# Sparse attention on one core: the parts of the keys stored once, 128 rows each, and doubled when they are loaded

## The chip, the core and the metric

The kernel runs on one core of one Trainium2 chip. The core has a tensor engine (PE; its weight loads are listed as PEld), a vector engine (DVE), a scalar engine (ACT), GpSimd (POOL) and a sync engine (SP) that here only issues DMAs. Each engine works through its own list of instructions in order. The metric is device time in microseconds for one execution of the whole program.

## The reference, cut to what matters

The program is a block of two transformer layers on 1024 tokens of width 1024, in float32. Layer 1 mixes the tokens in two ways: a sparse attention (`_dsa`, 8 heads of 64 channels; for each query the 256 keys with the largest indexer score) and a state-space scan (S5). The change touches the sparse attention's keys:

```python
def _mixer_dsa_s5(x, w_in, ...):
    h = x @ w_in
    q, k, v, qi, ki, wi, u = _split(h, L1_SPLITS)
    o_dsa = _dsa(q..., k..., v..., qi..., ki, wi * (IDX_HEADS ** -0.5))
    ...
def one_block(args):                       # in _dsa, 128 queries at a time
    logits = jnp.einsum('bqhd,bsd->bqhs', qii, k_idx) * (IDX_DIM ** -0.5)
    score = jnp.einsum('bqhs,bqh->bqs', jax.nn.relu(logits), wi)
    score = jnp.where((key_pos[None, :] <= qpos[:, None])[None], score, -jnp.inf)
    _, sel = lax.top_k(score, topk)        # 256 keys
    s = jnp.einsum('bqhd,bqkhd->bhqk', qi, gather(k, sel)) * (dh ** -0.5)
    p = jax.nn.softmax(jnp.where(sel_ok[:, None], s, -jnp.inf), axis=-1)
    return jnp.einsum('bhqk,bqkhd->bqhd', p, gather(v, sel))
```

## The kernel before, in words

Each float32 factor is split into a high and a low part, so a product is two or three matmuls. The sparse attention does not gather: it computes all causal scores and adds a mask (`bias`, one for each block of 128 queries) that the indexer and the top-256 search made on DVE, ACT and POOL.

`l1_in` (line 1699) projects layer 1's inputs: first values and the scan's inputs, then for each of 4 pairs of heads the queries (`i` = 0) and the keys (`i` = 1), in two halves of 512 tokens. A projection writes 128 rows to PSUM: rows 0 to 63 are the pair's even head, rows 64 to 127 the odd one. ACT copies them as the high part `qkh`, DVE subtracts for the low part `qkl`. All of them go to DRAM and come back later, since on-chip memory is short.

The scores of a head contract over 128 rows. The query operand `qa` holds the head's 64 high rows and its 64 low rows; the key operand must hold the same 64 key rows twice, once against each. `ka` is such a doubled high part, `kl` a doubled low part, each 128 x 512. Before the change the doubling is done by the stores: SP stores each head's 64 rows twice into `dk` (lines 1740 to 1745), two DMAs for each part of 128 rows, and `dsa`'s `load` (line 1759) reads 128 different rows back.

`dsa` runs twice, for the first 512 queries (16 of the 48 key loads) and then for the last 512 (32 of them). The values `vv`, the queries `qa` and the keys are all loaded on POOL's DMA queue; weights (`wr`), the scan's tables (`s5tab`, `ut`) and the stores of `qkh` and `qkl` are issued by SP.

Line 471 stands in every row of the profile, because the program is not issued as written. The functions only record operations. A planner (class `Plan`, `order`, line 242) then simulates the engines with a cost for each operation (line 207) and picks the next one by priority; a DMA's cost there is a fixed issue time of its queue plus its output bytes at 360 bytes a nanosecond. It also assigns on-chip buffers as it goes, and `issue` (line 464) emits the result. So a DMA that is added, removed or made smaller changes the planned times, and with them the order of all that follows on every engine and which buffer each tile gets. On the chip the lists then run in order with semaphore waits; a load waits in POOL's list until the buffer's last reader is done.

Of the kernel before, what the change touches and what calls it, by code (L numbers as in the profile page):

```python
# [11 lines left out]
F32 = mybir.dt.float32  # L12
# [461 lines left out]
P, T, N, KD = 128, 1024, 512, 8  # L474
# [42 lines left out]
class Kern:  # L517
# [1181 lines left out]
    def l1_in(self, x, dq, dk, dv, du):  # L1699

        V, S, A, nc = self.V, self.S, self.A, self.nc
        W = A["l1_fm"]
        us = [self.unit(A["l1_v"][i]) for i in range(4)]
        for b in range(8):
            ps = self.ps1((P, 8, 64))
            bs = slice((b % 4) * P, (b % 4 + 1) * P)
            self.tm(us, lambda k: tuple(t[:, bs] for t in x[k][b // 4]), ps)
            for hg in range(2):
                v = self.slab(F32R, "vv", (P, 4, 2, 64))
                for par in range(2):  # L1710
                    src = ps[:, hg * 4 + par:hg * 4 + 4:2, :]
                    hs, ls = v[:, par::2, par, :], v[:, par::2, 1 - par, :]
                    self.copy(S, hs, src)
                    V.tensor_tensor(ls, src, hs, ALU.subtract)
                nc.scalar.dma_start(out=dv[b, hg], in_=v.rearrange("p a b c -> p (a b c)").bitcast(F32))
            yield
        us = [self.unit(A["l1_u"][i]) for i in range(4)]
        for h in range(2):

            uq = [self.slab(name="ut", shape=(P, 8, 4, 16)) for _ in range(4)]  # L1720
            for j in range(4):
                ps = self.ps1((P, 4, 8, 16))
                self.tm(us, lambda k: tuple(t[:, j::4] for t in x[k][h]), ps)
                for q in range(4):
                    self.copy(S, uq[q][:, :, j, :], ps[:, q])
                    if j == 3:
                        nc.scalar.dma_start(out=du[q, h], in_=uq[q].rearrange("p a b c -> p (a b c)"))
                yield
        for pr in range(4):
            for i, w in enumerate((5 + pr, 9 + pr)):  # L1730
                u = self.unit(W[w])
                for h in range(2):
                    ps = self.ps1()
                    self.dense(x, h, ps, lambda k: self.blk(u, k))
                    hi, lo = self.slab(F32R, "qkh"), self.slab(F32R, "qkl")
                    f = 1.0 if i else 0.125
                    S.activation(hi, ps, AF.Copy, scale=f)
                    V.scalar_tensor_tensor(lo, ps, f, hi, op0=ALU.mult, op1=ALU.subtract)
                    A, B = slice(0, 64), slice(64, 128)
                    st = nc.sync.dma_start  # L1740
                    if i:
                        for part, t in enumerate((hi, lo)):
                            for odd, src in enumerate((A, B)):
                                st(out=dk[pr, h, part, odd].rearrange("(r p) n -> p r n", r=2),
                                   in_=t[src].bitcast(F32)[:, None, :].to_broadcast([64, 2, N]))
                    else:
                        q = dq[pr, h].rearrange("o p n -> (o p) n")
                        st(out=q[0:64], in_=hi[A].bitcast(F32))
                        st(out=q[64:192], in_=lo.bitcast(F32))
                        st(out=q[192:256], in_=hi[B].bitcast(F32))  # L1750
                    yield

    def dsa(self, dq, dk, dv, bias, mix, h):

        V, S, G, TE = self.V, self.S, self.G, self.TE
        val, qk, og = {}, {}, {}
        ld = G.dma_start

        def load(pr):

            if pr % 2 == 0:
                for b in range(4 * h + 4):
                    v = self.slab(F32R, "vv")
                    ld(out=v, in_=dv[b, pr // 2])
                    val[pr // 2, b] = v
            for odd in range(2):
                q = self.slab(F32R, "qa")
                k, l = ([self.slab(F32R, n) for c in range(h + 1)] for n in ("ka", "kl"))
                ld(out=q, in_=dq[pr, h, odd])
                for c in range(h + 1):  # L1770
                    ld(out=k[c], in_=dk[pr, c, 0, odd])
                    ld(out=l[c], in_=dk[pr, c, 1, odd])
                qk[pr, odd] = q, k, l

        def item(hd):
            pr, odd = divmod(hd, 2)

            def prep():
                if odd == 0:
                    load(pr)  # L1780

            def score(qb, w, p):
                q, k, l = qk[pr, odd]
                qs, nm = slice(qb % 4 * P, (qb % 4 + 1) * P), None
                for c in range(0, w, N):
                    n, s = min(N, w - c), self.ps1()
                    m, o = max(n, 256), slice(c, c + n)
                    TE.matmul(s[:, :m], q[:, qs], k[c // N][:, :m], start=True, stop=False)
                    TE.matmul(s[:, :m], q[:, qs], l[c // N][:, :m], start=False, stop=True)
                    last, nm = nm, self.small(1, "nm")  # L1790
                    V.tensor_tensor_reduce(out=p[:, o], in0=s[:, :n], in1=bias[qb][:, o], scale=-1.0,
                                           scalar=-NEG if last is None else last, op0=ALU.add, op1=ALU.min, accum_out=nm)
                return p, nm, -1.0

            def emit(po, sums):
                if not odd:
                    og[h] = self.slab(name="og")
                self.fold(po, odd, og[h], sums)
                if odd:
                    self.dump("o_dsa", og[h], (pr, slice(None), slice(h * N, h * N + N)))  # L1800
                    hi, lo = self.slab(F32R, "mh"), self.slab(F32R, "ml")
                    self.split(og[h], hi, lo, self.by("dsao_h"), self.by("dsao_l"))
                    mix[pr][h] = (hi, lo)

            return hd, h, prep, score, lambda kb: val[hd // 4, kb][:, (hd % 4) * P:(hd % 4 + 1) * P], emit

        yield from self.attention([item(hd) for hd in range(8)])
# [338 lines left out]
def build(ctx, tc, A, out, dbg=None, stop=None):  # L2146

    drams = ctx.enter_context(tc.tile_pool(name="dram", bufs=1, space=DRAM)), {}
    with ExitStack() as first:
        K = Kern(first, tc, A, out, dbg, drams)  # L2150
        program(K, A, out, stop)
        plan = K.nc
        order = plan.order()
        made = K.tiles
    K = Kern(ctx, tc, A, out, dbg, drams, plan.places, made)
    program(K, A, out, stop)
    K.nc.issue(tc, order, plan.took)
    return plan, K.nc


def program(K, A, out, stop=None):
# [19 lines left out]
    dt = K.dram("dt", [4, 2048, P])  # L2181
    dr = K.dram("dr", [KD, P, T])
    dq = K.dram("dq", [4, 2, 2, P, N])
    dk = K.dram("dk", [4, 2, 2, 2, P, N])
    dv = K.dram("dv", [8, 2, P, N])
    du = K.dram("du", [4, 2, P, N])

# [209 lines left out]
```

## Time and profile before

| | |
|---|---|
| time, median of 3 runs | 2381.92 us (2379.25 to 2382.75) |
| time of the profiled execution | 2390.38 us |
| its span (first to last instruction) | 2388.6 us |
| granted TensorE clock, mean | 0.99 |
| PE busy | 2305.8 us, 97% |
| DVE, ACT, POOL busy | 1768.3, 1330.8, 468.2 us (74%, 56%, 20%) |
| DMA moved | 356.59 MB, 174939 packets |
| POOL's DMA queue (q0) | 12672 packets, 23.07 MB, 3.6% of 16 engines |
| SP's DMA queue (q1) | 110704 packets, 243.81 MB, 31.9% |

Read it from the top: PE is busy for 97% of the span, so only work of PE, or time in which PE stands still, can move the end. The page's 40 slices show where it stands still: its digit is 9 everywhere but in the first slice, the last, and two in a row that read 7 and 8, about 1433 to 1552 us. Keys are stored from 1365 to 1470 us and loaded from 1441 to 1597 us.

### The profile page before, as it was taken

Reading aid. Unit: us, or ns where it says so; the run is one execution under the profiler, and the core shown is the slowest. Engines: PE = TensorE matmul, PEld = TensorE weight load, DVE = VectorE, ACT = ScalarE, POOL = GpSimd, SP = SyncE. Lnnn points to the kernel's source line nnn. Section 1 sums busy time; section 2 is a strip of 40 time slices with the busy share of each in tenths; the row PEclk is TensorE's granted clock in tenths of the full one; section 3 lists DMA queues with packets and bytes.
Section 4 is the critical chain, followed back from the end, with each engine's and each line's share of the span. In section 5 each row is a group of like instructions: output and inputs, shape, how many; then the busy total and the mean of one; then the engine's idle time right before and its main releaser. Section 6 shows DMA issues by size and latency. Waiting matters only on the chain. (4 is left out here: it accounts for less than half of the span.)

```text
span 2388.6 us, 33377 instructions
## 1 busy us (share of the span) xinstructions
PE 2305.8 (97%) x11368; PEld 1910.2 (80%) x11368; DVE 1768.3 (74%) x3353; ACT 1330.8 (56%) x2648; POOL 468.2 (20%) x488
## 2 busy tenths in 40 slices
PE   8999999999999999999999997899999999999997
PEld 7788888887878788887778876788877787888887
DVE  8676778468776567579799989885587755675796
ACT  4365567437555554446578775775275455444463
POOL 1252332232000000003211235752320000000021
PEclk9999999999999999999999998999999999999998
DMA  5420001325654585655103469553155546665561
GB/s 182 170 80 1 1 1 51 101 71 162 204 168 154 190 299 194 207 189 203 67 36 115 145 204 282 155 157 127 53 166 187 168 146 212 225 253 193 178 238 36
DMA packets 174939, 356.59 MB, mean 149 GB/s; under 512 B 26784, under 2 KB 39344, under 8 KB 174768
## 3 DMA queue, kind: packets, MB, share of 16 engines
q1 hardware_dynamic: 110704, 243.81, 31.9%
q10 hardware_dynamic: 51392, 87.58, 9.9%
q0 software_dynamic: 12672, 23.07, 3.6%
q8 instruction: 89, 1.46, 0.3%
q14 instruction: 82, 0.67, 0.1%
HBM read 249.66 MB, written 104.73 MB: 148 GB/s over the span
## 5 line engine op out<-in xcount | busy, mean ns | idle before, releaser
L471 PE MATMUL PS<-bh,wb 128*128 128x512 f32 x1792 | 569.0, 395 | 14.5 <-ACT u L471 6.8
L471 PEld LDWEIGHTS PS<-bh,wb 128*128 128x128 f32 x1792 | 335.6, 188 | 105.1 <-ACT u L471 12.6
L471 PE MATMUL PS<-bl,wb 128*128 128x512 f32 x896 | 350.5, 391 | 0.0
L471 PE MATMUL PS<-gl,vh 128*128 128x512 f32 x832 | 324.0, 390 | 2.1 <-DVE gl L471 2.1
L471 PE MATMUL PS<-gh,vh 128*128 128x512 f32 x832 | 322.6, 391 | 2.5 <-ACT vh L471 1.8
L471 PE MATMUL PS<-gh,vl 128*128 128x512 f32 x832 | 323.7, 390 | 0.0
L471 PEld LDWEIGHTS PS<-bl,wb 128*128 128x128 f32 x896 | 169.2, 189 | 34.1
L471 PEld LDWEIGHTS PS<-gh,vh 128*128 128x128 f32 x832 | 156.1, 188 | 37.5 <-ACT vh L471 2.2
L471 PEld LDWEIGHTS PS<-gl,vh 128*128 128x128 f32 x832 | 156.2, 188 | 35.2 <-DVE gl L471 2.5
L471 PEld LDWEIGHTS PS<-gh,vl 128*128 128x128 f32 x832 | 156.2, 188 | 32.3
L471 POOL TENSOR_TENSOR wl<-wr,wh 128x512 fp32r<-128x512 f32 x77 | 120.8, 1584 | 254.9 <-ACT wh L471 154.4
L471 ACT ACTIVATE c<-c 128x512 f32<-128x512 f32 x224 | 140.7, 630 | 50.5 <-DVE c L471 43.5
L471 PE MATMUL PS<-xh,wh 128*128 128x512 f32 (+1 forms) x400 | 155.2, 393 | 12.7 <-ACT xh L471 6.7
L471 POOL TENSOR_TENSOR lnacc<-res,res 128x512 f32<-128x512 f32 (+1 forms) x8 | 9.8, 1223 | 768.1 <-DVE res L471 740.9
L471 ACT ACTIVATE gh<-hr 128x512 fp32r<-128x512 f32 x208 | 129.2, 623 | 52.1 <-PE PS L471 32.6
L471 PE MATMUL PS<-xh,wl 128*128 128x512 f32 (+1 forms) x400 | 154.1, 388 | 2.8 <-POOL wl L471 2.8
L471 DVE TENSOR_TENSOR gl<-hr,gh 128x512 fp32r<-128x512 f32 x208 | 147.7, 711 | 10.9 <-PE PS L471 5.2
L471 PE MATMUL PS<-xl,wh 128*128 128x512 f32 (+1 forms) x400 | 155.3, 389 | 0.0
L471 ACT ACTIVATE wb<-wf 128x512 fp32r<-128x512 f32 x96 | 59.7, 628 | 153.2 <-DMA wf<-in_l_w 94.0
L471 DVE TENSOR_TENSOR wb<-s,wb 128x512 fp32r<-128x512 f32 x128 | 87.8, 688 | 77.0 <-ACT wb L471 76.9
L471 DVE TENSOR_TENSOR vl<-s,vh 128x512 fp32r<-128x512 f32 x112 | 84.2, 754 | 78.5 <-ACT vh L471 39.9
L471 ACT ACTIVATE vh<-s 128x512 fp32r<-128x512 f32 x112 | 70.2, 629 | 108.3 <-PE PS L471 73.2
(371 smaller groups left out, 5497.5 us busy)
## 6 DMA issues: line engine op xcount, KB each, us to landing
wr<-in_l_w SPq DMA_DIRECT2D x118, 512.0 KB, 5.3
hr<-hd SPq DMA_DIRECT2D x208, 256.0 KB, 3.4
wf<-in_l_w SPq DMA_DIRECT2D x80, 512.0 KB, 3.8
hd<-t ACTq DMA_DIRECT2D x128, 256.0 KB, 2.7
hd<-c ACTq DMA_DIRECT2D x96, 256.0 KB, 2.3
wr<-in_l_fm SPq DMA_DIRECT2D x25, 512.0 KB, 5.3
wr<-in_l_wo SPq DMA_DIRECT2D x16, 512.0 KB, 4.5
dx<-res ACTq DMA_DIRECT2D x32, 256.0 KB, 2.4
```

What stands on the lines that cost most here:

```text
L471: r = getattr(queue.real, method)(*a, **k)
```

## The change

`l1_in` stores each part of a key projection as it is, 128 rows, with one DMA: 16 stores to `dk` where there were 32, 4.2 MB where there were 8.4. `load` still issues 48 key loads of 256 KB on POOL's queue, but the source of each is now one head's 64 rows with a first dimension of 2 and a step of 0, so the load reads the 64 rows twice. The buffers that are filled are the same as before.

```diff
--- before.py
+++ after.py
@@ -1740,9 +1740,7 @@
                     st = nc.sync.dma_start
                     if i:
                         for part, t in enumerate((hi, lo)):
-                            for odd, src in enumerate((A, B)):
-                                st(out=dk[pr, h, part, odd].rearrange("(r p) n -> p r n", r=2),
-                                   in_=t[src].bitcast(F32)[:, None, :].to_broadcast([64, 2, N]))
+                            st(out=dk[pr, h, part], in_=t.bitcast(F32))
                     else:
                         q = dq[pr, h].rearrange("o p n -> (o p) n")
                         st(out=q[0:64], in_=hi[A].bitcast(F32))
@@ -1768,8 +1766,8 @@
                 k, l = ([self.slab(F32R, n) for c in range(h + 1)] for n in ("ka", "kl"))
                 ld(out=q, in_=dq[pr, h, odd])
                 for c in range(h + 1):
-                    ld(out=k[c], in_=dk[pr, c, 0, odd])
-                    ld(out=l[c], in_=dk[pr, c, 1, odd])
+                    for part, t in enumerate((k[c], l[c])):
+                        ld(out=t, in_=dk[pr, c, part, 64 * odd:64 * odd + 64][None].to_broadcast([2, 64, N]))
                 qk[pr, odd] = q, k, l
 
         def item(hd):
@@ -2181,7 +2179,7 @@
     dt = K.dram("dt", [4, 2048, P])
     dr = K.dram("dr", [KD, P, T])
     dq = K.dram("dq", [4, 2, 2, P, N])
-    dk = K.dram("dk", [4, 2, 2, 2, P, N])
+    dk = K.dram("dk", [4, 2, 2, P, N])
     dv = K.dram("dv", [8, 2, P, N])
     du = K.dram("du", [4, 2, P, N])
```

The planner reorders the program between about 1366 and 1650 us; elsewhere the lists are the same. Three places are shown: before, then after. In all three the names are tile or DRAM names with buffer numbers, and 64x2x512 is a shape.

SP, around the second to last weight of the pair projections (`wr_3230`, 512 KB) and the stores of a key projection (`dk`):

```order
L471 DMA s5tab_3203_7770<-ds_149 64x512 x2
L471 DMA s5T_3204_7771<-dt_150 128x8x128
L471 DMA dk_153<-qkh_3185_7774 64x2x512 x2
L471 DMA dk_153<-qkl_3186_7776 64x2x512 x2
L471 DMA wr_3230_7778<-in_l1_fm 128x1024
L471 DMA dq_152<-qkh_3217_7780 64x512 x2
L471 DMA dq_152<-qkl_3218_7781 128x512
```

```order
L471 DMA dk_153<-qkh_3169_7765 128x512
L471 DMA s5tab_3203_7767<-ds_149 64x512 x2
L471 DMA dk_153<-qkl_3170_7766 128x512
L471 DMA s5T_3204_7769<-dt_150 128x8x128
L471 DMA wr_3230_7774<-in_l1_fm 128x1024
L471 DMA dk_153<-qkh_3185_7773 128x512
L471 DMA dk_153<-qkl_3186_7776 128x512
```

The weight stood behind the four stores of `qkh_3185` and `qkl_3186`, and now stands ahead of the two that are left of them. Fifteen rows later the last weight, `wr_3261`, moves in the same way from behind the query store `dq<-qkl_3254` to a place ahead of it.

DVE, at the end of the projections; `eq`, `lt`, `cs` and `bias` make the masks of the last four query blocks, `wl` is the low part of the last weight, `wr_3261`:

```order
L471 TENSOR_TENSOR SM_5516<-SM_5516 128x4
L471 TENSOR_SCALAR eq_3177_7819<-sc_2685_7584,SM_5516 128x640
L471 TENSOR_SCALAR lt_3176_7820<-sc_2685_7584,SM_5516 128x640
L471 SCALAR_TENSOR_TENSOR cs_3179_7822<-oneb_6491,eq_3177_7819 128x640
L471 TENSOR_SCALAR eq_3181_7827<-sc_2724_7592,SM_5516 128x768
L471 SCALAR_TENSOR_TENSOR eq_3177_7819<-cs_3179_7822,SM_5516,eq_3177_7819 128x640
L471 SCALAR_TENSOR_TENSOR cs_3183_7831<-oneb_6491,eq_3181_7827 128x768
```

```order
L471 TENSOR_SCALAR SM_5516<-SM_5516 128x4
L471 TENSOR_TENSOR wl_3263_7823<-wr_3261_7813,wh_3262_7819 128x512
L471 TENSOR_TENSOR SM_5516<-SM_5516 128x4
L471 TENSOR_TENSOR wl_3265_7826<-wr_3261_7813,wh_3264_7821 128x512
L471 TENSOR_SCALAR eq_3177_7829<-sc_2685_7584,SM_5516 128x640
L471 TENSOR_SCALAR lt_3176_7831<-sc_2685_7584,SM_5516 128x640
L471 SCALAR_TENSOR_TENSOR cs_3179_7833<-oneb_6491,eq_3177_7829 128x640
```

The two `wl` operations were POOL's before; they are now DVE's, and stand ahead of the mask chain.

PE, in the first half of the second run of `dsa`; `p` transposes and `pth`, `ptl` products belong to the head before, `ka_3587` and `kl_3589` are keys loaded by POOL:

```order
L471 MATMUL PS_5517<-ident_5522,p_3527_7993 128x128 x2
L471 MATMUL PS_5517<-ka_3587_8002,qa_3586_7999 128x512
L471 MATMUL PS_5517<-ident_5522,p_3530_8000 128x128
L471 MATMUL PS_5517<-ident_5522,p_3527_7993 128x128
L471 MATMUL PS_5517<-ident_5522,p_3530_8000 128x128 x3
L471 MATMUL PS_5517<-kl_3589_8006,qa_3586_7999 128x512
L471 MATMUL PS_5517<-pth_3535_7995,vv_3404_7864 128x256
```

```order
L471 MATMUL PS_5517<-ptl_3548_8018,vv_3406_7872 128x256
L471 MATMUL PS_5517<-pth_3547_8015,vv_3407_7876 128x256
L471 MATMUL PS_5517<-ptl_3548_8018,vv_3407_7876 128x256
L471 MATMUL PS_5517<-ka_3587_8005,qa_3586_8002 128x512
L471 MATMUL PS_5517<-kl_3589_8007,qa_3586_8002 128x512
L471 MATMUL PS_5517<-pth_3565_8020,vv_3404_7864 128x256
L471 MATMUL PS_5517<-ka_3587_8005,qa_3586_8002 128x512
```

The first scores with `ka_3587` and `kl_3589` move behind the products of the head before, to where their later scores stood; further on, `ka_3592`'s first scores move the other way, from behind the transposes and the scan's matmuls that follow `kl_3590`'s scores to right behind those scores.

## Rows read from the trace of the kernel before

**Rows 1.** The page's first lines: the span, then busy time of each engine, its share of the span and its instructions.

```profile
span 2388.6 us, 33377 instructions
...
PE 2305.8 (97%) x11368; PEld 1910.2 (80%) x11368; DVE 1768.3 (74%) x3353; ACT 1330.8 (56%) x2648; POOL 468.2 (20%) x488
```

**Rows 2.** Windows of the core: the stretch (us from the span's start), its length, then busy time and instructions of each engine, the clock granted to TensorE as a share of full speed (1.00 is the level of 2.4 GHz, 0.50 would be 1.2 GHz throughout), the mean busy share of the 16 DMA engines, GB/s.

```profile
1400.00:1500.00 100.00, 83.90 (x422) 67.13 (x421) 92.02 (x202) 63.59 (x146) 56.61 (x59) 0.92 0.83 234
1440.00:1450.00 10.00, 5.24 (x32) 4.25 (x31) 8.01 (x15) 3.63 (x7) 4.58 (x5) 0.84 1.17 350
1450.00:1460.00 10.00, 9.72 (x35) 7.48 (x34) 8.29 (x9) 0.00 (x0) 6.11 (x8) 0.79 1.00 270
```

**Rows 3.** Timeline of PE, 1405 to 1470 us, the matmuls that waited. Columns: start us, duration us, engine, line, operation, output and inputs, type and count; in brackets how long the engine had been idle before, and what ended it.

```profile
1409.19 0.50 PE L471 MATMUL PS<-xh,wh 128*128 128x512 f32 x1 [0.70 <-ACT wh L471]
...
1410.55 0.51 PE L471 MATMUL PS<-xh,wl 128*128 128x512 f32 x1 [0.62 <-POOL wl L471]
...
1445.88 0.50 PE L471 MATMUL PS<-xh,wh 128*128 128x512 f32 x1 [2.20 <-ACT wh L471]
...
1449.27 0.79 PE L471 MATMUL PS<-xh,wl 128*128 128x512 f32 x1 [1.88 <-POOL wl L471]
...
1464.95 0.38 PE L471 MATMUL PS<-ka,qa 128*128 128x256 f32 x1 [1.27 <-DVE qkl L471]
```

**Rows 4.** Timeline of SP's DMA issues, 1395 to 1440 us; the columns are the same (the duration is that of the issue, xN that of N in a row).

```profile
1400.81 2.31 SPq L471 DMA_DIRECT2D dk<-qkl  x2
1403.16 0.67 SPq L471 DMA_DIRECT2D wr<-in_l_fm  x1
...
1436.93 0.54 SPq L471 DMA_DIRECT2D dq<-qkl  x1
1437.57 0.37 SPq L471 DMA_DIRECT2D wr<-in_l_fm  x1
```

**Rows 5.** Timeline, first of ACT (one row), then of DVE, 1440 to 1465 us: the use of the last projection weight, and the chain that makes the four masks.

```profile
1445.19 1.15 ACT L471 ACTIVATE wh<-wr 128x512 fp32r<-128x512 f32 x2 [2.33 <-DMA wr<-in_l_fm]
...
1441.16 0.60 DVE L471 TENSOR_SCALAR eq<-sc,SM 128x640 bf16<-128x640 f32 x1
1443.23 0.56 DVE L471 TENSOR_SCALAR lt<-sc,SM 128x640 bf16<-128x640 f32 x1 [1.47 <-DMA dq<-qkl]
...
1448.07 1.49 DVE L471 TENSOR_TENSOR bias<-lt,eq 128x640 bf16<-128x640 bf16 x1
1450.10 0.62 DVE L471 TENSOR_SCALAR lt<-sc,SM 128x768 bf16<-128x768 f32 x1 [0.53 <-PE PS L471]
...
1452.66 0.69 DVE L471 TENSOR_SCALAR eq<-sc,SM 128x896 bf16<-128x896 f32 x1 [1.01 <-PE PS L471]
1453.94 0.56 DVE L471 TENSOR_TENSOR bias<-lt,eq 128x768 bf16<-128x768 bf16 x1 [0.59 <-PE PS L471]
...
1456.35 1.64 DVE L471 TENSOR_SCALAR lt<-sc,SM 128x896 bf16<-128x896 f32 x1
...
1464.22 0.68 DVE L471 SCALAR_TENSOR_TENSOR qkl<-PS,qkh 128x512 fp32r<-128x512 f32 x1
```

**Rows 6.** The page's DMA parts: a queue (packets, MB, share of 16 engines' span; q0 carries what POOL issues), then DMA issues (output and input, queue, operation, count, KB each, median us from issue to landing).

```profile
q0 software_dynamic: 12672, 23.07, 3.6%
...
wr<-in_l_fm SPq DMA_DIRECT2D x25, 512.0 KB, 5.3
...
vv<-dv POOLq DMA_DIRECT2D x24, 256.0 KB, 3.4
ka<-dk POOLq DMA_DIRECT2D x24, 256.0 KB, 4.1
kl<-dk POOLq DMA_DIRECT2D x24, 256.0 KB, 4.1
...
qa<-dq POOLq DMA_DIRECT2D x16, 256.0 KB, 4.4
```

**Rows 7.** Timeline of POOL's key loads with little time before their use (first four rows), and of PE where their buffers come free or their matmuls run.

```profile
1514.44 0.53 POOL L471 DMA_DIRECT2D kl<-dk  x1
...
1524.18 0.54 POOL L471 DMA_DIRECT2D kl<-dk  x1
...
1528.69 0.54 POOL L471 DMA_DIRECT2D ka<-dk  x1
...
1577.77 0.53 POOL L471 DMA_DIRECT2D kl<-dk  x1 [2.31 <-PE PS L471]
...
1515.86 0.40 PE L471 MATMUL PS<-kl,qa 128*128 128x512 f32 x1
...
1523.22 0.39 PE L471 MATMUL PS<-kl,qa 128*128 128x512 f32 x1
...
1529.64 0.28 PE L471 MATMUL PS<-kl,qa 128*128 128x256 f32 x1
...
1531.74 0.28 PE L471 MATMUL PS<-kl,qa 128*128 128x256 f32 x1
...
1533.41 0.41 PE L471 MATMUL PS<-s5tab,s5x 128*128 128x128 f32 x2
...
1581.70 0.63 PE L471 MATMUL PS<-kl,qa 128*128 128x512 f32 x2
...
1583.42 0.51 PE L471 MATMUL PS<-ka,qa 128*128 128x256 f32 x2 [0.52 <-DMA ka<-dk]
```

## The prediction

> **What bounds the kernel now.** Start with the busy times: PE works for 97% of the span, the other engines for far less [rows 1]. An edit that touches no PE work, as this one, can only move the end by changing how long PE stands still. So the second view is the windows: between 1400 and 1500 us PE is busy for 83.9 of 100 us, at a mean granted clock of 0.92 [rows 2], and that is where keys are stored and loaded. The third view is PE's timeline there, which names what each wait ended on. The reader is to see two chains. One begins at a weight: PE waits for the high and low part of a projection weight (0.70 and 0.62 us near 1410, 2.20 and 1.88 us near 1447) [rows 3], ACT makes the high part when the weight has landed [rows 5], and SP issues that weight behind other DMAs [rows 4]. The other ends in the first scores, where PE waits 1.27 us for the last `qkl` [rows 3]; DVE makes it behind the four masks [rows 5]. Key loads hardly matter: the one wait that ends on a key load is 0.52 us, at 1583 [rows 7].
>
> **The stores.** 16 stores of 256 KB go, from a queue that is no bound: SP computes nothing, and no wait of PE in these rows ends on a store. Two low-part stores cost 2.31 us of issue [rows 4]; their removal is worth nothing by itself and is hidden under PE. It counts only through what stands behind them in SP's list, which is the next part. If it gave more, it would be through a less busy DMA system (share 1.17 in 1440 to 1450 [rows 2]), but no key store is issued in that window.
>
> **The weights on SP's queue.** `wr_3230` was issued at 1403.16, behind stores that began before 1400.81 [rows 4]. The new order puts it ahead of them, so it leaves at least 2.3 us earlier, and both waits that it causes, 0.70 and 0.62 us [rows 3], go: 1.3 us. What is late next there is nothing that these rows show. The last weight, `wr_3261`, passes the query store that stood at 1436.93 and leaves some 0.6 us earlier (1437.57 less 1436.93) [rows 4]. Together the last weight is in place 1.9 us earlier.
>
> **The mask chain.** Before, the chain began at 1441.16 and reached `qkl` at 1464.22, 23.1 us later. Of that 1.47 + 0.53 + 1.01 + 0.59 = 3.6 us were idle, so 19.5 us of work [rows 5]. Two operations in it are long: a `bias` of 1.49 us where the next one took 0.56, and an `lt` of 1.64 us where its neighbour took 0.62 [rows 5]; both ran when POOL made `wl`. With `wl` on DVE these 1.9 us should shrink away, which leaves 17.5. In the new order the chain stands behind the two `wl`, so it starts when the weight has landed, plus 1.15 us of ACT, plus one DVE subtraction, about the 0.68 us of the `qkl` row [rows 5]: 1.8 us, and `qkl` starts 19.4 us after the landing. Before it started 1464.22 - 1445.2 = 19.0 us after it. So 0.3 to 0.4 us of the 1.9 are lost: the reorder is worth **1.6 us**. If the long operations stay long it is a loss of 0.4; if the weight also lands faster, more (a rival, below).
>
> **The loads.** Their number, bytes and queue stay. What is new is the shape of the source: 2 by 64 rows, where it was 128. No row of before has such a source: a load's price must be bounded from both sides. POOL issued 24 + 24 + 24 + 16 = 88 loads of 256 KB in 12672 packets [rows 6], 144 each: one for each of 128 rows and 16 more, which is what one closing packet on each of 16 engines would give. A packet takes 0.036 x 16 x 2388.6 / 12672 = 0.109 us [rows 1, 6], so an engine's 8 rows of one load take 0.9 us of the 4.1 us to landing [rows 6]. The low end: the rows are still spread over 16 engines, nothing changes, or at best the landing falls to 3.4 us, that of `vv` at the same size [rows 6]. The high end: the rows are shared out by the source's first dimension, which is now 2. Then two engines carry 64 rows each, 7.0 us instead of 0.9, and a load lands after about **10.2 us** instead of 4.1. I take the high end, since both sides of all those loads had a first dimension of 128, that is what gave each engine its equal share, and the new source no longer has it; but the rows do not decide it, and the low end keeps nearly half the chance.
>
> The Trainium skill ("DMA: Bandwidth & Descriptors", section "Rules for kernel authors") has a rule that speaks against this change: the number of engines follows the slowest dimension of both patterns, and a leading zero-stride broadcast of c copies confines a DMA to at most c. By that rule the high end holds. The same page ("Why a DMA increments its semaphore by 16 and not by 1") notes that some direct copies which GpSimd issues get all 16 engines on this chip; by that exception the low end holds. No run here shows either yet.
>
> **What late loads cost.** Most key loads are issued 9 us or more ahead of their use, or PE reaches them only behind one of the waits below. Four are tight:
> - `kl_3589`, issued at 1514.44 before, used in the new order at the place of 1523.22; its buffer comes free with the matmul at 1515.86 [rows 7]. 7.4 us of slack: 2.8 us late.
> - `kl_3590`, issued at 1524.18. By the old places it has 5.5 us (1529.64), by the new first use up to 7.5 (1531.74) [rows 7]. I take 6.4, the middle: 3.8 us late.
> - `ka_3592`, issued at 1528.69; its use moves forward to about 1533.41 [rows 7]. 4.7 to 5.0 us of slack, 5.2 late, of which 3.8 have already been waited for: 1.4.
> - a `kl` issued at 1577.77 and used at 1581.70, 3.9 us [rows 7]: 6.3 us late; the `ka` that PE waited for at 1583.42 then falls into the same wait.
>
> PE waits in order, so these add: 2.8 + 3.8 + 1.4 + 6.3 = **14.3 us**. With a landing of 3.4 + 6.1 they are 12.2. If those two engines also serve other queues' packets half the time, each load is 3.5 us later still, four times: 28. POOL itself may take longer to issue the new shape; at 0.53 us each [rows 7] even a third more is 8 us over 48 loads on an engine that is busy for 20%, hidden under PE in all but the tight places.
>
> **The sum.** The profiled execution took 2390.38 us (span 2388.6), 8.5 above the median of 2381.92. 2390.4 - 1.6 + 14.3 = 2403.1 for the same execution, or **2394.6** against the median.
>
> **The rivals.**
> - A, no slower: the loads keep their 16 engines. Then only the reorder is left, 2381.9 - 1.6 = 2380.3 us. For it: 144 packets a load is a count that needs no particular shape. Against it: the equal shares of before came with a first dimension of 128.
> - B, faster: as A, and the weight at the head of the mask chain no longer lands late. It took from 1437.57 to about 1445.2, 7.6 us [rows 4, 5], against the 5.3 us that these 512 KB weights take at the median [rows 6]: 2.3 more. With the two waits of 2.20 and 1.88 us shortened, PE keeps working and the clock stays up; in 1440 to 1460 it was granted 0.84 and 0.79 [rows 2], which is (0.16 + 0.21) x 10 / 0.5 = 7.4 us at the lower level, worth half of that, 3.7. Together 1.6 + 2.3 + 3.7 = 7.6: 2374.3 us. It decides if `wr_3261` lands before about 1441 in the old times. Against it: the DMA share there is 1.17, of transfers that stay.
> - C, far slower: all key loads use the same two engines. 48 x 7.0 = 336 us of them between 1441 and 1597, 156 us: 180 us more, 2562 us. Against it: nothing ties successive loads to one pair.
> - The stores' saving as such, the 4.2 MB, does nothing in any of these cases: they lie under PE.
>
> The Trainium skill's section on the 16 increments says that a software queue's smaller transfers take their engines round-robin; by that, C falls.
>
> **How the numbers follow.** The forecast, late loads on two engines, gets 0.55; A 0.24, B 0.18, C 0.03. The forecast's own range is 2386 (the reorder between 1500 and 1650 gives 4 us back, and loads land at the lower bound) to 2410 (28 us late). A reaches from 2377 to 2383, B to 2374. Leaving out the lower half of B (0.09), C and the top of the forecast (together 0.1) gives 2375 to 2410. A measurement of this kernel can tell about 0.2%, 4.8 us, from no change. Faster: B and the low edge of A, 0.21. Same: the rest of A and the forecast's lowest edge, 0.24. Slower: 0.55.
>
> **What would show it.** Right: the landing of `ka` and `kl` near 10 us where `vv` stays at 3.4; PE waits of 1 to 6 us that end on `ka<-dk` or `kl<-dk` near 1520, 1530 and 1580; no wait for `wh` or `wl` near 1410. The loads' step is wrong if they still land in about 4 us. The weights' step is wrong if PE still waits for `wl` near 1410, the mask chain's if the first scores begin later than 19.4 us after the last weight lands. The whole is wrong if PE's waits on keys sum to under 5 us.

## The result: slower by 33.6 us

| | before | changed |
|---|---|---|
| median of 4 runs, us | 2382.34 | 2415.9 (2410.5 to 2419.69) |
| ratio | | 1.0132, 95% interval 1.0107 to 1.0157 |
| profiled execution, us (span) | 2390.38 (2388.6) | 2412.78 (2410.9) |

The direction was forecast; the time lies above the range (2375 to 2410). First the page of the changed kernel, the lines that answer to [rows 1] and [rows 6], with the line that counts the packets and the landings of the key and query loads:

```profile
span 2410.9 us, 33374 instructions
...
PE 2311.3 (96%) x11368; PEld 1918.2 (80%) x11368; DVE 1770.3 (73%) x3355; ACT 1330.0 (55%) x2645; POOL 477.5 (20%) x489
...
DMA packets 215642, 352.56 MB, mean 146 GB/s; under 512 B 69536, under 2 KB 82096, under 8 KB 215472
...
q0 software_dynamic: 55680, 23.25, 5.4%
...
vv<-dv POOLq DMA_DIRECT2D x24, 256.0 KB, 3.9
ka<-dk POOLq DMA_DIRECT2D x24, 256.0 KB, 11.3
kl<-dk POOLq DMA_DIRECT2D x24, 256.0 KB, 11.6
qa<-dq POOLq DMA_DIRECT2D x16, 256.0 KB, 10.6
```

The reader is to see a count: POOL's queue carries the same loads and nearly the same bytes in 55680 packets, where it had 12672 [rows 6]. The 40 loads of `vv` and `qa` have 144 packets each, as before, 5760. That leaves 49920 for 48 key loads, 1040 each: 128 rows, 16 closing packets and 896 more, which is 14 x 64. By this count two engines carry 64 rows each, and each of the other 14 gets 64 packets too, of almost no bytes (no view names the engine of a packet; the page counts 42752 more packets under 512 B; the 16 stores that are gone take away 16 each). This is the high end of the forecast's bounds: the key loads land after 11.3 to 11.6 us, where 10.2 was expected.

PE's busy time grew by 5.5 us with the same 11368 matmuls, and its idle time (span less busy) from 82.8 to 99.6 us. Next PE's timeline, all waits on key loads of 0.25 us or more, in the columns of [rows 3]; the trace's view of all that touches `dk` sums PE's waits on them, the small ones included, to 22.1 us (0.5 before):

```profile
1463.97 0.58 PE L471 MATMUL PS<-kl,qa 128*128 128x256 f32 x1 [0.90 <-DMA kl<-dk]
...
1500.55 0.39 PE L471 MATMUL PS<-kl,qa 128*128 128x256 f32 x1 [0.94 <-DMA kl<-dk]
...
1527.08 0.47 PE L471 MATMUL PS<-ka,qa 128*128 128x512 f32 x1 [0.64 <-DMA ka<-dk]
1528.21 0.50 PE L471 MATMUL PS<-kl,qa 128*128 128x512 f32 x1 [0.66 <-DMA kl<-dk]
...
1539.52 0.55 PE L471 MATMUL PS<-ka,qa 128*128 128x256 f32 x1 [5.29 <-DMA ka<-dk]
...
1542.24 0.58 PE L471 MATMUL PS<-kl,qa 128*128 128x256 f32 x1 [2.17 <-DMA kl<-dk]
...
1557.05 0.79 PE L471 MATMUL PS<-kl,qa 128*128 128x512 f32 x1 [4.24 <-DMA kl<-dk]
...
1560.10 1.01 PE L471 MATMUL PS<-kl,qa 128*128 128x256 f32 x2 [0.96 <-DMA kl<-dk]
...
1583.16 0.36 PE L471 MATMUL PS<-ka,qa 128*128 128x256 f32 x1 [1.12 <-DMA ka<-dk]
...
1606.22 0.70 PE L471 MATMUL PS<-ka,qa 128*128 128x512 f32 x2 [3.48 <-DMA ka<-dk]
...
1608.62 1.22 PE L471 MATMUL PS<-kl,qa 128*128 128x512 f32 x2 [1.15 <-DMA kl<-dk]
...
1611.20 0.79 PE L471 MATMUL PS<-ka,qa 128*128 128x256 f32 x2 [0.29 <-DMA ka<-dk]
```

### The profile page after: what moved, and what is told of

Its sections match the earlier page's. It is cut to its first block, busy times and chain, and to the rows that moved or that the text cites. A ratio compares the mean times of both kernels' runs of the same rounds, so it can differ in the third digit from the quotient of the medians.

```text
span 2410.9 us, 33374 instructions
## 1 busy us (share of the span) xinstructions
PE 2311.3 (96%) x11368; PEld 1918.2 (80%) x11368; DVE 1770.3 (73%) x3355; ACT 1330.0 (55%) x2645; POOL 477.5 (20%) x489
## 3 DMA queue, kind: packets, MB, share of 16 engines
q0 software_dynamic: 55680, 23.25, 5.4%
```

## The experiments

All times are medians, ratios go to runs of the kernel before on the same chip.

**Is it the source's shape or the order?** Two kernels take the change apart. The first keeps the order and the stores of before, instruction for instruction, and changes the loads alone:

```diff
-                    ld(out=k[c], in_=dk[pr, c, 0, odd])
-                    ld(out=l[c], in_=dk[pr, c, 1, odd])
+                    ld(out=k[c], in_=dk[pr, c, 0, odd][0:64][None].to_broadcast([2, 64, N]))
+                    ld(out=l[c], in_=dk[pr, c, 1, odd][0:64][None].to_broadcast([2, 64, N]))
```

> The order and the doubled stores of before, all of them; only the source of each of the 48 key loads is 64 of the doubled rows, read twice with a first dimension of 2. Theory T (a source whose first dimension is 2 puts a load's data on two DMA engines): landing of ka and kl near 11 us, and most of the loss is here without any reorder: 2407 to 2420 us. Rival R (the new order of the program makes the loss): landing near 4 us and 2382, as before. Rival S (the single stores, which the key loads now follow more closely): 2382 as well.

Measured: 2411.96 us against 2383.91, ratio 1.0119 (1.0092 to 1.0146); 55680 packets, `ka` lands after 10.7 us, PE waits 21.9 us on keys. Theory T holds, R and S fall: in the old order the shape alone costs 28 us. PE's 11368 matmuls stand in the same order in both traces.

The second keeps the order of the changed kernel and gives the loads a first dimension of 64:

```diff
-ld(out=t, in_=dk[pr, c, part, 64 * odd:64 * odd + 64][None].to_broadcast([2, 64, N]))
+ld(out=t, in_=dk[pr, c, part, 64 * odd:64 * odd + 64]
+   .rearrange("(a m) n -> a m n", a=64)[:, None].to_broadcast([64, 2, 1, N]))
-ld(out=q, in_=dq[pr, h, odd])
+ld(out=q, in_=dq[pr, h, odd].rearrange("(r a m) n -> a r m n", r=2, a=64))
```

> The changed kernel with its own order and its single stores; each key load still reads 64 rows twice, but row by row: the first dimension is 64 (step one row), the second 2 (step 0), so the two copies of a row land on neighbouring partitions. The queries' loads read their 64 high and 64 low rows interleaved in the same way. T: landing back at about 4 us, no PE wait on keys over 1 us, and the time is the forecast's reorder alone: 2376 to 2384 us. Rival R: the order is that of the changed kernel, so 2410 to 2420. Rival U (reading a row twice is what is slow, whatever the shape): landing near 11 us and 2410 to 2420.

Measured: 2385.49 us, ratio 1.0005 (0.9992 to 1.0018). Its page, in the same lines:

```profile
span 2382.8 us, 33374 instructions
...
PE 2302.9 (97%) x11368; PEld 1909.9 (80%) x11368; DVE 1767.2 (74%) x3355; ACT 1329.5 (56%) x2645; POOL 470.4 (20%) x489
...
q0 software_dynamic: 12672, 23.07, 3.6%
...
ka<-dk POOLq DMA_DIRECT2D x24, 256.0 KB, 4.0
kl<-dk POOLq DMA_DIRECT2D x24, 256.0 KB, 4.1
qa<-dq POOLq DMA_DIRECT2D x16, 256.0 KB, 3.8
```

It reads each row twice with a step of 0, in the changed kernel's order (PE's matmuls are the same, one by one), from single stores, and no difference to before can be told; the median lies 1.5 us above T's range. R and U fall; the reorder's forecast gain of 1.6 us lies inside the interval and can't be told.

**Is it the size of the first dimension, and how does it grow?** Three kernels in the order of before read 128 different rows in 2, 4 or 8 groups; nothing is read twice:

```diff
+                rows = lambda t: t.rearrange("(m a) n -> a m n", a=2)   # 4, 8
-                ld(out=q, in_=dq[pr, h, odd])
+                ld(out=q, in_=rows(dq[pr, h, odd]))
-                    ld(out=k[c], in_=dk[pr, c, 0, odd])
+                    ld(out=k[c], in_=rows(dk[pr, c, 0, odd]))
```

(and `l[c]` likewise.)

> The kernel before, its order and its doubled stores; every key load reads 128 different rows, none twice, but in two groups (the even rows of the stored block, then the odd ones), so that the first dimension of the source is 2 with a step of one row. The 16 query loads read in the same groups. Theory T (the size of the first dimension decides): as slow as with the two copies: landing near 11 us, 2410 to 2425 (16 more loads are slow). Rival Z (the step of 0, reading the same rows twice, decides): landing 4.1 us, 2382.

> As the one with a first dimension of 2, with four groups of 32 rows. T: four engines carry 32 rows each, 3.2 + 32 x 0.109 = 6.7 us to landing; only loads with under 6.7 us of slack are late: 2384 to 2395. Z: 2382.

> As the one with a first dimension of 2, with eight groups of 16 rows. T: eight engines carry 16 rows each, 3.2 + 16 x 0.109 = 4.9 us to landing, 0.8 over before; the two or three tightest loads are late by under 1 us: 2381 to 2386. Z: 2382.

| first dimension | us | ratio (interval) | `ka` landing, us | q0 packets | PE waits on keys, us |
|---|---|---|---|---|---|
| 128 (before) | 2384.98 | 1 | 4.1 | 12672 | 0.5 |
| 8 | 2389.71 | 1.0023 (1.0008 to 1.0038) | 6.2 | 20864 | 5.8 |
| 4 | 2409.55 | 1.01 (1.0062 to 1.0137) | 9.0 | 37248 | 21.3 |
| 2 | 2429.96 | 1.0185 (1.0163 to 1.0207) | 10.9 | 70016 | 25.8 |

The queue's lines and the key landings of the kernels with 8, 4 and 2, one fence each:

```profile
q0 software_dynamic: 20864, 23.11, 4.7%
...
ka<-dk POOLq DMA_DIRECT2D x24, 256.0 KB, 6.2
```

```profile
q0 software_dynamic: 37248, 23.17, 5.3%
...
ka<-dk POOLq DMA_DIRECT2D x24, 256.0 KB, 9.0
```

```profile
q0 software_dynamic: 70016, 23.30, 5.6%
...
ka<-dk POOLq DMA_DIRECT2D x24, 256.0 KB, 10.9
```

Z falls: no row is read twice. The packets fit one formula in all of them. With k engines a load has 128 rows, (16 - k) times 128 / k empty packets and 16 closing ones: 272, 528 and 1040 packets for k = 8, 4 and 2. For 64 such loads and 24 of `vv`, 3456 + 64 x 272 = 20864, and 37248 and 70016 in the same way, to the packet. The landings are longer than expected, 6.2 for 4.9 and 9.0 for 6.7 us: the expectations count one load by itself, and here several lie in the queue. All three times lie above their ranges; the loss at 4 was 25 us where at most 10 were expected. How a load's time grows with those ahead of it was not measured by itself.

**Where is it lost?** Rows first, but one of `dsa`'s two runs keeps the two-copy source:

```diff
+                a = 64 if h == 1 else 1        # 1: the two-copy source; the other kernel has h == 0
```

> As the kernel with rows first, but the 16 key loads of the first run (the first 512 queries) keep the source with a first dimension of 2. The forecast put all of its 14.3 us at four loads of the second run; by that this kernel costs under 3 us more than the one with rows first: 2378 to 2386. Rival V (the first run pays too, through the first scores and what ACT and DVE wait for there): 8 to 14 us more, 2386 to 2396.

> As the kernel with rows first, but the 32 key loads of the second run (the last 512 queries) keep the source with a first dimension of 2. The forecast's own term: 14 us more than the one with rows first, about 2394. Rival V: 18 to 25 us, 2398 to 2405, since places with more slack than four fall late as well once the queue behind the key loads is late.

Measured: 2388.18 us with the slow first run (ratio 1.002, 1.0008 to 1.0032), 2.7 more than rows first; 2406.03 with the slow second run (1.0093, 1.0073 to 1.0113), 20.5 more, with PE waits on keys of 16.6 us. So most of the loss lies in the second run, as forecast, and is larger than forecast: by the differences V holds for the second run and not for the first, though 2388.18 lies in V's range and not in the other. Both together cost 30.4 us (2415.9 - 2385.49), 7 more than the sum of the two, though each median moves by some us.

**Is it that loads are late against their order, or that the engines are too slow?** One kernel tells the planner of the late landing, one moves the query loads to SP's queue, and one gives that last order fast loads:

```diff
-                        end = dma + 1500
+                        end = dma + 1500 + (7000 if ops[i][3]["in_"].shape[0] == 2 else 0)
```

```diff
-                ld(out=q, in_=dq[pr, h, odd])
+                self.nc.sync.dma_start(out=q.bitcast(F32), in_=dq[pr, h, odd])
```

> The changed kernel, its two-copy loads unchanged, but the planner's model has a key load land 7.0 us later, as on the chip; so it orders the program for late keys. Theory L (what hurts is that each load is late against an order made for early ones; the two engines have room enough): ka and kl still land in about 11 us, PE waits on keys shrink from 22 us to under 10, 2390 to 2403. Rival B (two engines can't carry the loads fast enough, or the loads slow everything else down): the waits move but stay, 2410 to 2420.

> The changed kernel, its two-copy key loads unchanged, with the 16 query loads issued by SP instead of by POOL (the planner reorders around them). If the loss beyond the forecast comes from query loads that land late behind key loads in one queue (10.6 us against 4.4 before): qa back to 3 to 5 us and 5 to 10 us faster than the changed kernel, 2406 to 2411. If the late keys alone are the loss: 2413 to 2419, with qa early and PE waiting for keys as long as before.

> The kernel with the query loads on SP, its order unchanged, but each key load reads row by row (first dimension 64). If that order is better of itself, and this is why it lost only 13 us to before: 2370 to 2378. If the order is only kinder to late keys: 2380 to 2387, and the late keys cost 10 to 18 us in it against 30 in the changed kernel's order.

Measured: with the planner told, 2408.89 us (1.0095, 1.0076 to 1.0113); PE waits on keys fall to 11.3 us, but the time only by 7: neither L nor B as stated. With the queries on SP, 2397.69 us (1.0055, 1.0036 to 1.0074); keys still land after 11.6 us, but PE waits on them for 3.2. It beat the range given, and `qa` landed after 6.8 us, not 3 to 5. The same order with fast loads: 2386.63 us (1.0008, 0.9995 to 1.0021). So it is no better order of itself; it is kinder to late keys. The same late landing costs 28 us in the order of before, 30 in that of the changed kernel and 11 in this one. In the profiled executions 7.9 us of this are one wait before the first scores, with slow loads, then with fast ones:

```profile
1467.61 0.55 PE L471 MATMUL PS<-ka,qa 128*128 128x256 f32 x1 [10.03 <-DMA vv<-dv]
```

```profile
1460.44 0.36 PE L471 MATMUL PS<-ka,qa 128*128 128x256 f32 x1 [2.13 <-DMA qa<-dq]
```

This matmul reads no `vv`, so the first row's releaser is doubtful. It needs the query load that SP issued at 1456.52, 11 us before. So the late loads cost time through SP's queue too; more on that below.

**Two repairs.** Rows first with the queries stored interleaved, in two stores instead of three; and two loads of 64 rows for each key operand:

```diff
+                        q = q.rearrange("(p r) n -> r p n", r=2)
+                        st(out=q[0], in_=hi.bitcast(F32))
+                        st(out=q[1], in_=lo.bitcast(F32))
```

```diff
+                        for r in range(2):
+                            ld(out=t[64 * r:64 * r + 64], in_=dk[pr, c, part, 64 * odd:64 * odd + 64])
```

> Rows first, with the queries interleaved where they are stored, in two stores of 128 rows where three were needed, and loaded as they lie; the planner orders it anew. Keys land at 4 us. SP's 24 query stores become 16, which lie under PE: 2380 to 2387, no difference to before that can be told. If the projection weights behind these stores come early enough to matter, 2374 to 2378.

> The single stores of the changed kernel; each key operand is loaded by two DMAs of the same 64 rows, 128 KB each, one to each half of the partitions, so no dimension of 2 is left (96 key loads; the planner orders anew). T: all 16 engines carry each, landing near 4 us, no PE wait on keys over 2 us. The 48 more issues are 48 x 0.53 = 25 us of POOL, mostly hidden: 2380 to 2392. If POOL's issues decide in the tight places: 2392 to 2405.

Measured: 2384.9 us (0.9991, 0.998 to 1.0001), no difference to before that can be told; keys land in 3.9 us. The half loads: 2403.19 us (1.0088, 1.0064 to 1.0112), though `ka` lands after 4.2 us and PE waits on keys for 3.8 us only. The planner ordered 96 loads quite differently, and PE's waits there are spread over DVE and ACT; that POOL's issues decide is not shown, though the time lies in that range. Nothing here beats the kernel before.

## Why the prediction was right in its cause and wrong in its size

**The loads: right.** The high end was taken and holds: packet counts show 64 rows on each of two engines. The Trainium skill ("DMA: Bandwidth & Descriptors", section "Rules for kernel authors") states that rule, and all four counts above agree with it. The exception in the same page's section "Why a DMA increments its semaphore by 16 and not by 1", that some direct copies issued by GpSimd get all 16 engines, does not show in any load here whose first dimension is 2, 4 or 8. 10.2 us to landing was mis-sized by 1.1 to 1.4 at the median, and by much more where many transfers are under way. That the landing of `qa` would rise from 4.4 to 10.6 us was not foreseen; a query load lies in the same queue right behind or ahead of key loads.

**What late loads cost: the step that failed.** The term was 14.3 us, PE's waits in four places. Measured are 22.1 us of waits on keys, and 28.1 us of time against rows first, which has the same order with fast loads. At `kl_3589` 0.64 + 0.66 where 2.8 were forecast; at `kl_3590` and the `ka` ahead of it 5.29 + 2.17 for 3.8; at `ka_3592` nothing for 1.4; at the `kl` of 1577 and its neighbours 3.48 + 1.15 + 0.29 for 6.3. Those four sum to 13.7, near 14.3 by luck: each place is off by 1.4 to 3.7 us. The rest, 8.4 us, is at loads of which the prediction said that they are issued 9 us or more ahead, or that PE reaches them only behind one of its waits. Both halves of that sentence fail.

The first half fails because landing took longer than 10.2 us there. The `kl` loads that ended PE's waits at 1464 and 1500 were issued at 1445.80 and 1480.34, 18.2 and 20.2 us before PE went on; for the waits at 1560 and 1583 it is 12.5 and 13.6 us. These four waits are 0.90 + 0.94 + 0.96 + 1.12 = 3.9 us. The second half fails because a wait of PE gives the next load no more room when that load's issue moves with it, as at 1557 (4.24 us). POOL's timeline, first the two early loads, then 1529 to 1546 us:

```profile
1445.80 0.79 POOL L471 DMA_DIRECT2D kl<-dk  x1 [4.94 <-PE PS L471]
...
1480.34 0.83 POOL L471 DMA_DIRECT2D kl<-dk  x1
...
1530.41 0.78 POOL L471 DMA_DIRECT2D kl<-dk  x1 [1.89 <-PE PS L471]
...
1544.77 1.29 POOL L471 TENSOR_TENSOR ml<-og,mh 128x512 fp32r<-128x512 f32 x1 [6.25 <-ACT mh L471]
1545.99 0.84 POOL L471 DMA_DIRECT2D kl<-dk  x1
```

The load at 1530.41 is `kl_3590`: it waited for PE to free its buffer, and landed in PE's wait of 2.17 us. The load at 1545.99 stood in POOL's list behind an operation that waited 6.25 us for ACT. ACT waited for DVE, and DVE for PE's first scores, that is, for the same late keys:

```profile
1542.86 0.35 DVE L471 CUSTOM_DVE_ANT_0 p<-PS,bias,SM 128x128 f32<-128x128 f32 x1 [6.25 <-PE PS L471]
```

```profile
1543.25 0.83 ACT L471 ACTIVATE p<-p,SM 128x640 f32<-128x640 f32 x1 [9.11 <-DVE SM L471]
```

PE reached that load's scores 6.8 us after its issue and then waited 4.24 us, at 1557. With rows first the same load was issued at 1529.37 and used at 1535.56, 6.2 us later, without a wait. So PE's waits of 5.29 and 2.17 us just before gave it only 0.6 us more room. This load was not among the four.

**Other queues: left out.** The prediction had two engines that serve others too, but priced this for key loads alone. The trace's DMA view of 1436 to 1480 us, changed kernel, then rows first (packets and bytes, then landings):

```profile
DMA packets 17834, 10.66 MB, mean 242 GB/s; under 512 B 12394, under 2 KB 13418, under 8 KB 17831
...
s5tab<-ds SPq DMA_DIRECT2D x9, 256.0 KB, 11.7
...
ka<-dk POOLq DMA_DIRECT2D x6, 256.0 KB, 15.4
...
dk<-qkh SPq DMA_DIRECT2D x2, 256.0 KB, 11.0
```

```profile
DMA packets 11507, 13.27 MB, mean 302 GB/s; under 512 B 4906, under 2 KB 5930, under 8 KB 11504
...
s5tab<-ds SPq DMA_DIRECT2D x10, 256.0 KB, 6.9
ka<-dk POOLq DMA_DIRECT2D x7, 256.0 KB, 6.1
...
dk<-qkh SPq DMA_DIRECT2D x2, 256.0 KB, 6.4
```

The transfers shown land later in the changed kernel, SP's stores and tables with them. The two kernels differ in the sources of the key and query loads alone, so these slow the others; that it comes from sharing the two engines is the likely reason, but no view names a packet's engine. ACT's next operation needed a buffer that a key store was still reading, and PE waited behind it, in the changed kernel:

```profile
1470.60 0.63 ACT L471 ACTIVATE s5g<-s5yt 128x512 f32<-128x512 f32 x1 [12.26 <-DMA dk<-qkh]
```

```profile
1471.67 0.48 PE L471 MATMUL PS<-ident,p 128*128 128x128 f32 x1 [5.19 <-ACT p L471]
```

The kernel with only the first run slow has the same ACT wait, 11.59 us, and PE waits 4.51 us behind it, though that kernel is only 2.7 us slower than rows first. With the planner told it is 13.26 us, and 6.44 us of PE; that this is why that kernel stayed slow is not shown. With rows first neither wait is there.

**The clock: left out.** Windows of 1400 to 1700 us, changed kernel, then rows first, columns as in [rows 2]:

```profile
1400.00:1500.00 100.00, 80.30 (x407) 66.50 (x405) 87.73 (x192) 60.09 (x139) 51.50 (x54) 0.90 0.91 192
1500.00:1600.00 100.00, 78.82 (x505) 68.07 (x505) 75.92 (x203) 66.67 (x143) 64.01 (x69) 0.90 0.63 124
1600.00:1700.00 100.00, 92.75 (x524) 79.58 (x523) 61.83 (x149) 55.42 (x105) 35.94 (x35) 0.97 0.59 135
```

```profile
1400.00:1500.00 100.00, 84.36 (x459) 70.55 (x458) 94.01 (x213) 63.98 (x150) 55.55 (x62) 0.93 0.72 202
1500.00:1600.00 100.00, 93.55 (x614) 80.48 (x613) 89.09 (x239) 79.79 (x166) 67.36 (x81) 1.00 0.60 167
1600.00:1700.00 100.00, 98.22 (x510) 82.79 (x509) 55.25 (x109) 42.49 (x79) 32.76 (x25) 1.00 0.26 90
```

With one level at half the other, (0.10 + 0.10 + 0.03) x 100 / 0.5 = 46 us were spent at 1.2 GHz, against 14. PE stood still more often there, and the same matmuls took 8.4 us longer (2311.3 against 2302.9; the figure is rough, since before, which lost nothing, has 2305.8). The forecast used the clock in rival B alone, as something to be won.

**The sum of it.** Changed kernel against rows first, same order, profiled executions: 2410.9 - 2382.8 = 28.1 us, of which 8.4 are slower matmuls and 19.7 idle time. PE's waits on keys differ by 22.1 - 0.8 = 21.3 us, and the wait for ACT at 1471 is 5.2 more: together 26.5, more than 19.7. A part of the loss comes back later. Counted from PE's 6400th matmul to its 8000th (1332 to 1633 us with rows first), the changed kernel takes 335.4 us for 301.4, 34.0 more, 9.4 of them busy; from there to the end it takes 7.9 us less. The kernel with only the first run slow takes 12.4 us more in that stretch and 7.1 less behind it. So in these executions the first run does pay, as V said, and more than half of it is won back. What gives it back is open.

**The weights and the mask chain: the waits went, the gain did not come.** The waits of 0.70 and 0.62 us went, but something else was late next, in the changed kernel:

```profile
1411.66 1.53 PE L471 MATMUL PS<-s5U,s5tab 128*128 128x128 f32 x11 [1.43 <-ACT s5U L471]
```

Before, the two waits there summed to 1.3 us [rows 3], so nothing was won. The mask chain's long operations shrank as expected (the `bias` from 1.49 to 0.47 us, the `lt` from 1.64 to 0.67), but `qkl` began at 1461.80, 20.1 us after the last weight was used at 1441.73. By the prediction's own sign (19.4 us) this step is wrong: it had no idle time in the chain, where 0.30 + 0.46 us were, and one DVE subtraction ahead of it, where both stand. The waits moved to the first scores:

```profile
1462.71 0.36 PE L471 MATMUL PS<-ka,qa 128*128 128x256 f32 x1 [4.17 <-DVE qkl L471]
```

It was 1.27 us there before [rows 3]. From 1440 us to the first scores PE's waits of 0.25 us or more, those on keys left out, sum to 7.0 us before, 6.1 now and 6.2 with rows first.

**The rivals.** A and B needed loads on 16 engines, and fell. C (one pair for all loads) fell too: 48 x 7.0 = 336 us of work, and the key loads were issued between 1437.8 and 1626.0. The stores' saving was worth nothing that can be told, as said: rows first has it, and is no faster than before.

## What to carry to other kernels

Look at the first dimension of a DMA's pattern, not only at its bytes (here the source's; the destination had 128 rows throughout): in a source that is doubled, put the rows first and the copies second, and choose the layout of the partner operand to match. When a load in a planned order becomes late, don't add the lateness of the tight places alone. A wait of PE can delay the issue of the next load, a load's landing grows with what else is under way, other queues land late too, and the clock was lower where PE paused. A change that lets a planner reorder is best tested with the order held fixed; here that took the layout of one more operand.

## What the runs showed of the hardware

- By the counts, a load confined to k engines gave each other engine as many packets as a carrying one has rows, of almost no bytes: 1040 packets for 256 KB at k = 2, 144 at k = 16. They are short: by the queue's shares (5.4% and 3.6% of 16 engines' span) the 43008 more packets took about 0.016 us each, an estimate, so 64 of them are 1.1 us and not the 7 us by which a load lands later.
- Its issue is longer too: POOL took 0.80 us (median) for a key load of two copies, 0.54 before and 0.59 to 0.60 with rows first, half more where a third was the guess. That is 13 us over 48 loads, on an engine that stayed busy for 20%.
- Eight engines are already worse than 16 by more than the share of rows says (6.2 us to landing against 4.1, where that share gives 4.9); between 1430 and 1600 us the mean busy share of the DMA engines was 0.91 with eight and 0.72 with 16.
